# Scan outputs read from PSUM, a skip term made by channel, and softmax maps combined by ScalarE and GpSimd, in a hybrid SSD and attention block

## The chip, the cores and the metric

The kernel runs on one core of a Trainium2 chip. Its metric is device time in microseconds (us); lower is better. Three runs of the kernel before stand at 1765.82, 1765.89 and 1776.22 us.

## The reference

One layer of a backbone block: a modulated norm, one input projection, and two groups of heads that read it side by side, a bidirectional scan (SSD) and a differential attention. Both go into an output projection, and a gated MLP follows. What the change touches is this, cut to its core (8 chunks of 128 tokens, 2 groups of 8 scan heads, 4 attention heads with two maps each, 1024 queries over 1280 keys):

```python
# scan, per direction: y = intra-chunk part + state part + skip
y_diag = einsum('bclsgr,bcsgrp->bclgrp', scores * decay * dt, xs)
y_off  = einsum('bclgn,bcgrpn,bclgr->bclgrp', cm, h_starts, exp(a_cum))
yd     = y_diag + y_off + d_skip * xs
ys     = rmsnorm((yd_forward + yd_backward) * silu(z), ssd_norm_g)
# attention: two maps per head
p = softmax(q @ k * scale, axis=-1)
w = p[:, :, 0] - lam * p[:, :, 1]
o = w @ v
```

## The kernel before

The program is written as one stream in Python; what one engine does next is the order in which its instructions come out, and a scheduler may move them, except TensorE's in the stages where `pin` holds them in program order. Each engine works through its own queue in order.

After the startup and the input projection (to about 440 us) TensorE alternates between attention and a filler, by a debt that `run` keeps: each attention step yields a gap, and the filler is run until its costs (0.65, S_COST, M_COST) have paid for it. First the filler is `zproj`, the projection for z; when it is used up it is `ssd`, the scan. What is left of the scan when attention ends runs in `ssd_rest`, inside `mixffn`, beside the norm of the attention's output (tiles o, dg, yo). Then the output projection and the MLP follow to the end.

**Attention** goes by tiles of 128 queries of one head, 32 in all. For each of the two maps TensorE makes scores (tile sc, one buffer of three PSUM banks), VectorE takes their row maximum (stat), ScalarE the exponentials (et), and only then can TensorE write the next sc. One tile behind, `weigh` makes the map difference out of the two et tiles: a reciprocal, a 128x1 factor, and one VectorE instruction over 128x1280. TensorE transposes the result in ten blocks (tr), ScalarE or VectorE copies these out (wt), and after every second tile TensorE multiplies by V (po).

**The scan** runs 11 state steps first (`bwd`, `fwd`: GpSimd weighs x into xw and decays the state into hb or H, TensorE makes s, VectorE adds it), then `main(c, g)` for 8 chunks and 2 groups, with a state step between chunks. One such unit: the score product scs (for both groups at once, copied to sc by ScalarE), G = G * sc on VectorE, two state products yo (forward and backward), each copied out of PSUM by ScalarE and scaled by GpSimd, or scaled straight from PSUM by VectorE, by the letters of ENG_B (beside attention) and ENG_R (in the rest); the skip term xd = xt * dsum; two sums; eight small products y; yg = y + the sums; a transpose yt; and yt * z into zc, which goes to DRAM (yd). The PSUM pool pm has three buffers that scs, yo, y, yt and s take in turn.

The two lines of the loop around the change that words can't carry:

```python
nc.vector.scalar_tensor_tensor(out=ex[0], in0=ex[1], scalar=st[:, 6:7], in1=ex[0], op0=ALU.mult, op1=ALU.add)
e = [{"p": nc.gpsimd, "d": nc.vector}[x] for x in (ENG_R if self.rest else ENG_B)]   # "pdppdp", "ppppdp"
```

## Time and profile before

| | |
|---|---|
| median of three runs | 1765.89 us |
| the profiled execution | 1772.42 us |
| its span | 1770.5 us |
| TensorE busy | 1590.3 us (90%) |
| VectorE busy | 1206.5 us (68%) |
| GpSimd busy | 842.9 us (48%) |
| ScalarE busy | 758.9 us (43%) |
| DMA, mean | 154 GB/s |

The profile is one execution on the chip. A matmul in float32 shows as two instructions, so that "x16" is eight products. PE is TensorE, DVE VectorE, ACT ScalarE, POOL GpSimd, SP the engine that issues DMAs. "<- DVE x" behind an idle time names what ended it. In this text the stretch from 440 to 900 us is cut into four: the z projection beside attention (445 to 622 us, tiles 0 to 15), the state steps beside attention (622 to 730, tiles 16 to 23), the chunks beside attention (730 to 841, tiles 24 to 31), and the rest of the scan (841 to 897).

### The profile page before, as it was taken

The numbers are of one execution on the slowest core, as the hardware profiler recorded it, in microseconds if no ns is written. First come the engines' busy times: TensorE is split into PE (matmuls) and PEld (weight loads), VectorE is DVE, ScalarE is ACT, GpSimd is POOL, SyncE is SP. The second block draws the span as 40 slices with busy tenths as digits, with TensorE's granted clock in tenths as the row PEclk, the third lists the DMA queues.
The fourth block names the chain that finished last, engine by engine and source line by source line (L and its number), as shares of the span: only waits on it lengthen the run. The fifth ranks groups of instructions, "written<-read, shape, count | busy, mean of one in ns | idle before, by whom it ended". The sixth has DMA issues, their size and how long they took to land. (4 is left out here: it accounts for less than half of the span.)

```text
span 1770.5 us, 21306 instructions
## 1 busy us (share of the span) xinstructions
PE 1590.3 (90%) x7588; PEld 1271.8 (72%) x7588; DVE 1206.5 (68%) x1593; ACT 758.9 (43%) x1409; POOL 842.9 (48%) x559
## 2 busy tenths in 40 slices
PE   5899989997899978988899995999999999999986
PEld 2697877885687855666467774778888887777765
DVE  3478843354565657777875568987677777798886
ACT  4433577542354423444444254433334334355352
POOL 2231587784010045566756576343333334566642
PEclk8999999999899988999999997999999999999987
DMA  8365866766422284645564331323322225753222
GB/s 300 113 225 197 268 208 234 269 214 193 131 83 82 77 283 166 175 152 158 182 208 153 120 102 36 113 95 113 113 102 101 95 102 176 285 179 123 81 74 95
DMA packets 138825, 273.34 MB, mean 154 GB/s; under 512 B 11984, under 2 KB 60544, under 8 KB 138208
## 3 DMA queue, kind: packets, MB, share of 16 engines
q1 hardware_dynamic: 138128, 271.03, 46.2%
q8 instruction: 60, 0.98, 0.2%
q0 software_dynamic: 592, 0.96, 0.2%
q14 instruction: 45, 0.37, 0.1%
HBM read 197.63 MB, written 74.32 MB: 154 GB/s over the span
## 5 line engine op out<-in xcount | busy, mean ns | idle before, releaser
L145 PE MATMUL pu<-T,whi 128*128 128x512 f32 x1232 | 383.5, 392 | 8.7 <-ACT whi L125 8.7
L145 PEld LDWEIGHTS pu<-T,whi 128*128 128x128 f32 x1232 | 233.0, 189 | 57.6 <-ACT whi L125 9.2
L126 POOL TENSOR_TENSOR wlo<-S,whi 128x512 fp32r<-128x512 f32 (+2 forms) x122 | 167.0, 1373 | 192.8 <-ACT whi L125 192.6
L145 PE MATMUL pu<-T,wlo 128*128 128x512 f32 x616 | 242.5, 394 | 16.7 <-POOL wlo L126 11.8
L126 POOL TENSOR_TENSOR wlo<-wraw,whi 128x512 fp32r<-128x512 f32 (+2 forms) x118 | 152.2, 1294 | 163.3 <-ACT whi L125 156.3
L145 PE MATMUL lat<-hl,w_hi 128*128 128x512 f32 x640 | 206.2, 399 | 0.9 <-DVE dtt L599 0.9
L145 PE MATMUL pd<-T,whi 128*128 128x512 f32 x560 | 178.9, 400 | 11.6 <-ACT whi L125 7.4
L814 DVE TENSOR_REDUCE stat<-sc 128x1 f32<-128x1280 f32 x64 | 95.2, 1488 | 109.3 <-PE sc L145 109.2
L126 POOL TENSOR_TENSOR w_lo<-w_raw,w_hi 128x1024 fp32r<-128x1024 f32 (+1 forms) x36 | 81.8, 2275 | 179.3 <-ACT w_hi L125 157.6
L125 ACT CAST whi<-wraw 128x512 fp32r<-128x512 f32 (+2 forms) x140 | 81.3, 582 | 197.4 <-PE pu L145 118.9
L145 PEld LDWEIGHTS pu<-T,wlo 128*128 128x128 f32 x616 | 116.5, 189 | 45.2 <-POOL wlo L126 13.4
L145 PEld LDWEIGHTS lat<-hl,w_hi 128*128 128x128 f32 x640 | 122.9, 192 | 26.8 <-DVE dtt L599 1.1
L145 PE MATMUL sc<-K,S 128*128 128x512 f32 (+1 forms) x384 | 101.2, 401 | 45.1 <-DMA K<-kd 23.6
L815 ACT ACTIVATE et<-sc,stat 128x1280 f32<-128x1280 f32 x64 | 85.1, 1330 | 130.0 <-DVE stat L814 111.8
L145 PEld LDWEIGHTS pd<-T,whi 128*128 128x128 f32 x560 | 107.6, 193 | 37.8 <-ACT whi L125 9.6
L125 ACT CAST whi<-S 128x512 fp32r<-128x512 f32 (+2 forms) x144 | 81.6, 573 | 119.2 <-PE pu L145 88.4
L145 PEld LDWEIGHTS sc<-K,S 128*128 128x128 f32 x384 | 76.1, 207 | 72.9 <-ACT et L815 30.0
L145 PE MATMUL lat<-hl,w_lo 128*128 128x512 f32 x320 | 127.8, 399 | 0.0
L145 PE MATMUL pd<-T,wlo 128*128 128x512 f32 x280 | 113.3, 405 | 7.3 <-POOL wlo L126 7.1
L1409 DVE SCALAR_TENSOR_TENSOR xf<-pd,modl,xf 128x512 f32<-128x512 f32 (+1 forms) x138 | 95.9, 727 | 14.1 <-PE pd L145 10.8
L542 ACT ACTIVATE R<-R,lna 128x128 f32<-128x128 f32 x256 | 78.1, 391 | 53.7 <-POOL R L538 48.5
L538 POOL TENSOR_TENSOR R<-R,never 128x1024 f32<-128x1024 f32 x32 | 80.5, 2529 | 41.0 <-DMA R<-atd 39.0
(285 smaller groups left out, 3410.3 us busy)
## 6 DMA issues: line engine op xcount, KB each, us to landing
wraw<-wUp SPq DMA_DIRECT2D x46, 512.0 KB, 3.2
wt<-wmB SPq DMA_DIRECT2D x32, 512.0 KB, 4.1
R<-atd SPq DMA_DIRECT2D x32, 512.0 KB, 5.4
stg<-gf_d SPq DMA_DIRECT2D x21, 768.0 KB, 4.8
w_raw<-wU SPq DMA_DIRECT2D x28, 512.0 KB, 5.0
gf_d<-T SPq DMA_DIRECT2D x11, 1024.0 KB, 4.2
K<-kd SPq DMA_DIRECT2D x32, 320.0 KB, 7.6
xt<-xtok SPq DMA_DIRECT2D x19, 512.0 KB, 5.2
```

Of the source, the lines that this page charges most:

```text
L125: nc.scalar.copy(hi, src)
L126: (lo_eng or nc.vector).tensor_tensor(out=lo, in0=src, in1=hi, op=ALU.subtract)
L145: self.pe(self.nc.tensor.matmul(out, lhsT=lhsT, rhs=rhs, start=start, stop=stop))
L538: nc.gpsimd.tensor_tensor(out=R[:, d], in0=R[:, d], in1=self.never[:, d].unsqueeze(1).broadcast_to([P, 8, P]), op=ALU.add)
L542: nc.scalar.activation(e, e, AF.Exp, bias=self.lna[:, d, i, h:h + 1], scale=1.0)
L814: nc.vector.tensor_reduce(out=st[:, c:c + 1], in_=sc, axis=AX.X, op=ALU.max, negate=True)
L815: nc.scalar.activation(et, sc, AF.Exp, bias=st[:, c:c + 1], accum_out=acc)
L1409: nc.vector.scalar_tensor_tensor(out=o, in0=ps, scalar=self.gate5[:, dt:dt + 1], in1=o, op0=ALU.mult, op1=ALU.add)
```

## The change

Three things are changed. First, in the scan VectorE reads every product from PSUM itself: scs is made for each group apart and multiplied into G straight from PSUM, the backward yo is scaled into t, the forward yo is scaled in place and added to t, and yt is multiplied by z from PSUM. ScalarE's copies sc, t and yt are gone, and so are GpSimd's scalings and sums; ENG_B, ENG_R and the second t buffer go with them. Second, the skip term is no longer made by token in the scan: the convolved x is also stored by channel (xct), `zproj` loads its half (xc, one buffer), multiplies it by the skip factor of the channel and by the gate on VectorE and stores it (zx), and the scan loads zx and adds it to zc on GpSimd as its last step. Third, the maps are combined in two steps: ScalarE scales the second et in place, and GpSimd adds it to the first; the 128x1 factor is made by a tensor_scalar instead of a scalar_tensor_tensor. et has four buffers instead of three, wt three instead of four, and the last wt copy moves from VectorE to ScalarE (WT_ENG).

```diff
-ENG_B = "ppppdp"
-ENG_R = "pdppdp"
-WT_ENG = "aad"
+WT_ENG = "aaa"
...
+                    if u < U_B:
+                        nc.sync.dma_start(self.xct[u], y[:, CTX:])
...
+                xc = zp.tile([P, 512], F32, name="xc", bufs=1)
+                nc.sync.dma_start(xc, self.xct[u][:, sl])
                 zo = zp.tile([P, 512], F32, name="zo")
                 nc.scalar.activation(zo, p, AF.Tanh, scale=0.5)
                 nc.vector.scalar_tensor_tensor(out=zo, in0=zo, scalar=1.0, in1=p, op0=ALU.add, op1=ALU.mult)
                 nc.sync.dma_start(self.zt[u][:, sl], zo)
+                nc.vector.scalar_tensor_tensor(out=xc, in0=xc, scalar=self.dsum[:, u:u + 1], in1=zo,
+                                               op0=ALU.mult, op1=ALU.mult)
+                nc.sync.dma_start(self.zx[u][:, sl], xc)
...
-            et = ap.tile([P, TOK], F32, name="et", bufs=3)
+            et = ap.tile([P, TOK], F32, name="et", bufs=4)
...
-            nc.vector.scalar_tensor_tensor(out=st[:, 6:7], in0=st[:, 5:6], scalar=self.nlam[:, 0:1],
-                                           in1=self.s0[:, qt, h:h + 1], op0=ALU.mult, op1=ALU.mult)
-            nc.vector.scalar_tensor_tensor(out=ex[0], in0=ex[1], scalar=st[:, 6:7], in1=ex[0], op0=ALU.mult, op1=ALU.add)
+            nc.vector.tensor_scalar(out=st[:, 6:7], in0=st[:, 5:6], scalar1=self.nlam[:, 0:1],
+                                    scalar2=self.s0[:, qt, h:h + 1], op0=ALU.mult, op1=ALU.mult)
+            nc.scalar.mul(ex[1], ex[1], st[:, 6:7])
+            nc.gpsimd.tensor_tensor(out=ex[0], in0=ex[0], in1=ex[1], op=ALU.add)
...
+            zx = sp.tile([P, 4, P], F32, name="zx", bufs=Z_BUFS)
+            nc.sync.dma_start(zx, self.zx[ks, :, cs].rearrange("k p t -> p k t"))
...
+                ps = self.pm.tile([P, P], F32, tag="mm", name="scs")
+                self.mm(ps, bl[:, g, :], cl[:, g, :])
+                nc.vector.tensor_tensor(out=G, in0=ps.unsqueeze(1).broadcast_to([P, 8, P]), in1=G, op=ALU.mult)
+                t = sp.tile([P, 8, HD], F32, name="t")
+                for d, st in ((1, hb), (0, self.Hf)):
                     po = self.pm.tile([P, 512], F32, tag="mm", name="yo")
                     self.mm(po, cl[:, g, :], st[:, xg])
-                    if e[d] is nc.gpsimd:
-                        nc.scalar.copy(t.rearrange("p h d -> p (h d)"), po)
-                    src = t if e[d] is nc.gpsimd else h3(po)
+                    nc.vector.tensor_tensor(out=t if d else h3(po), in0=h3(po), in1=ea, op=ALU.mult)
+                    if d == 0:
+                        nc.vector.tensor_tensor(out=flat(t), in0=po, in1=flat(t), op=ALU.add)
...
-            e.tensor_tensor(out=zc, in0=y, in1=zc, op=ALU.mult)
+            nc.vector.tensor_tensor(out=zc, in0=pt, in1=zc, op=ALU.mult)
+            nc.gpsimd.tensor_tensor(out=zc, in0=zc, in1=zx, op=ALU.add)
```

How this moves the queues shows at three places. Line numbers of the changed kernel are its own.

VectorE, one chunk beside attention, before (TENSOR_REDUCE is the maximum of an sc, et<-et the map difference):

```order
L814 TENSOR_REDUCE stat<-sc 128x1
L976 TENSOR_TENSOR G<-G,sc 128x1024 x2
L835 COPY wt_6056<-tr 128x2x128
L820 RECIPROCAL stat<-stat 128x1
L821 SCALAR_TENSOR_TENSOR stat<-stat,nlam,s_95 128x1
L823 SCALAR_TENSOR_TENSOR et<-et,stat 128x1280
L814 TENSOR_REDUCE stat<-sc 128x1
L994 TENSOR_TENSOR t_6082<-t_6082,xd 128x512
L999 TENSOR_TENSOR yg<-y,t_6082 128x512
```

VectorE, the same place in the changed kernel, the first of the chunk's two units:

```order
L819 TENSOR_REDUCE stat<-sc 128x1 x2
L978 TENSOR_TENSOR G<-scs,G 128x1024
L985 TENSOR_TENSOR t<-yo,acum 128x512
L985 TENSOR_TENSOR yo<-yo,acum 128x512
L825 RECIPROCAL stat<-stat 128x1
L987 TENSOR_TENSOR t<-yo,t 128x512
L826 TENSOR_SCALAR stat<-stat,nlam,s_95 128x1
L993 TENSOR_TENSOR yg<-y,t 128x512
L1005 TENSOR_TENSOR zc<-yt,zc 128x512
L978 TENSOR_TENSOR G<-scs,G 128x1024
L819 TENSOR_REDUCE stat<-sc 128x1
```

Five instructions of a unit read PSUM where two and a half did, the 128x1280 instruction is gone, and between two maxima there now stands a whole unit.

GpSimd, one chunk beside attention, before (xw and H are the state step):

```order
L914 TENSOR_TENSOR H_6408<-H_6205,cd 128x1024
L986 TENSOR_TENSOR t_6285<-t_6285,acum 128x512
L986 TENSOR_TENSOR t_6294<-t_6294,acum 128x512
L993 TENSOR_TENSOR t_6285<-t_6285,t_6294 128x512
L1016 TENSOR_TENSOR zc<-yt,zc 128x512
L986 TENSOR_TENSOR t_6337<-t_6337,acum 128x512
L991 TENSOR_TENSOR xd<-xt,c_dskp 128x512
L986 TENSOR_TENSOR t_6342<-t_6342,acum 128x512
L1016 TENSOR_TENSOR zc<-yt,zc 128x512
L993 TENSOR_TENSOR t_6337<-t_6337,t_6342 128x512
L908 TENSOR_TENSOR xw<-xt,dte 128x1024
```

GpSimd, one chunk beside attention in the changed kernel:

```order
L920 TENSOR_TENSOR H_6674<-H_6480,cd 128x1024
L829 TENSOR_TENSOR et<-et 128x1280
L1006 TENSOR_TENSOR zc<-zc,zx 128x512
L829 TENSOR_TENSOR et<-et 128x1280
L1006 TENSOR_TENSOR zc<-zc,zx 128x512
L914 TENSOR_TENSOR xw<-xt,dte 128x1024
```

Ten small instructions of the scan have become two, and two additions of 128x1280 for the attention have come in.

VectorE beside the z projection, in the changed kernel (before, zo stands there without xc, and et<-et after the 128x1 factor):

```order
L825 RECIPROCAL stat<-stat 128x1
L826 TENSOR_SCALAR stat<-stat,nlam,s_95 128x1
L123 TENSOR_TENSOR wt_4306<-tr,wt_4305 128x2x128
L775 SCALAR_TENSOR_TENSOR zo<-zo,pz 128x512
L777 SCALAR_TENSOR_TENSOR xc<-xc,c_dskp,zo 128x512
L819 TENSOR_REDUCE stat<-sc 128x1 x2
```

The product xc has come in ahead of a maximum. On the queue of DMAs, a store of zx has come in between the first zt and the loads of the first head's S and K.

## Rows read from the trace of the kernel before

**Rows 1.** Busy time per stretch; columns: stretch, length, PE, PEld, DVE, ACT, POOL, granted clock, DMA share, GB/s

```profile
445.00:622.00 177.00, 164.88 (x888) 138.72 (x886) 109.22 (x139) 79.59 (x134) 10.60 (x4) 0.96 0.32 94
622.00:730.00 108.00, 85.19 (x348) 60.53 (x349) 72.08 (x77) 35.85 (x60) 54.49 (x29) 0.86 0.70 217
730.00:841.00 111.00, 98.49 (x520) 75.88 (x520) 86.90 (x85) 47.96 (x83) 74.64 (x55) 0.97 0.49 156
841.00:897.00 56.00, 46.00 (x213) 25.93 (x211) 46.09 (x68) 25.53 (x54) 38.88 (x27) 0.97 0.49 158
```

**Rows 2.** TensorE's waits from 440 to 900 us: total, times, longest

```profile
PE sc L145 <- DMA K<-kd: 23.6, 6, 10.5
PE sc L145 <- ACT et L815: 21.0, 13, 3.3
PE yt L1010 <- DVE yg L999: 9.2, 7, 3.7
```

**Rows 3.** VectorE's groups from 440 to 900 us, shapes apart: busy, mean ns, idle before

```profile
L814 DVE TENSOR_REDUCE stat<-sc 128x1 f32<-128x1280 f32 x64 | 95.2, 1488 | 109.3 <-PE sc L145 109.2
L823 DVE SCALAR_TENSOR_TENSOR et<-et,stat 128x1280 f32<-128x1280 f32 x32 | 61.1, 1908 | 0.6
L994 DVE TENSOR_TENSOR t<-t,xd 128x512 f32<-128x512 f32 x16 | 24.1, 1505 | 7.7 <-POOL t L993 7.7
L976 DVE TENSOR_TENSOR G<-G,sc 128x1024 f32<-128x1024 f32 x16 | 23.9, 1534 | 4.9 <-ACT sc L973 4.9
...
L821 DVE SCALAR_TENSOR_TENSOR stat<-stat,nlam,s 128x1 f32<-128x1 f32 x32 | 16.7, 521 | 0.9
L999 DVE TENSOR_TENSOR yg<-y,t 128x512 f32<-128x512 f32 x16 | 10.9, 682 | 0.5
```

**Rows 4.** Timeline, two engines at 789.7 us: start, length, instruction

```profile
789.66 1.90 POOL L914 TENSOR_TENSOR H<-H,cd 128x1024 f32<-128x1024 f32 x1
790.09 1.48 DVE L821 SCALAR_TENSOR_TENSOR stat<-stat,nlam,s 128x1 f32<-128x1 f32 x1
```

**Rows 5.** Timeline of TensorE, one pair of tiles, from 767 to 796 us

```profile
767.83 1.47 PE L145 MATMUL sc<-K,S 128*128 128x512 f32 x6 [2.23 <-ACT et L815]
...
776.11 1.41 PE L145 MATMUL sc<-K,S 128*128 128x512 f32 x6
777.36 1.02 PE L145 MATMUL yo<-H,cl 128*128 128x512 f32 x2
...
779.08 1.98 PE L145 MATMUL y<-xt,G 128*128 128x64 f32 x16
781.59 0.66 PE L1010 MATMUL yt<-c_masks,yg 128*128 128x128 f32 x4 [0.53 <-DVE yg L999]
782.00 1.41 PE L145 MATMUL sc<-K,S 128*128 128x512 f32 x6
...
784.12 1.88 PE L145 MATMUL s<-xw,btk 128*128 128x512 f32 x4
...
786.50 1.43 PE L145 MATMUL sc<-K,S 128*128 128x512 f32 x6 [0.28 <-ACT et L815]
787.77 4.48 PE L145 MATMUL po<-wt,V 128*128 128x256 f32 x20
794.48 1.43 PE L145 MATMUL sc<-K,S 128*128 128x512 f32 x6 [2.23 <-ACT et L815]
```

**Rows 6.** GpSimd's groups, shapes apart, whole span: busy, mean ns, idle before

```profile
L126 POOL TENSOR_TENSOR w_lo<-w_raw,w_hi 128x1024 fp32r<-128x1024 f32 x28 | 70.0, 2502 | 172.2 <-ACT w_hi L125 150.4 <-PE tr L831 21.7
...
L1016 POOL TENSOR_TENSOR zc<-yt,zc 128x512 f32<-128x512 f32 x16 | 20.8, 1302 | 7.5 <-ACT yt L1013 7.5
```

**Rows 7.** ScalarE's exponential, a group of its own, from 100 to 920 us

```profile
L815 ACT ACTIVATE et<-sc,stat 128x1280 f32<-128x1280 f32 x64 | 85.1, 1330 | 130.0 <-DVE stat L814 111.8 <-DMA K<-kd 16.8
```

**Rows 8.** Timeline at 555 us: a tile's reciprocal, and its first transposes

```profile
555.10 0.17 DVE L820 RECIPROCAL stat<-stat 128x1 f32<-128x1 f32 x1 [0.23 <-ACT et L815]
...
562.36 0.82 PE L831 MATMUL tr<-c_masks,et 128*128 128x128 f32 x6
```

More of the change, by code (lines that the diff above doesn't have):

```diff
@@ L61 @@
 Z_BUFS = 2
-T_BUFS = 2
 S_COST = 3.4
@@ L259, in build @@
             self.pa = self.pool(e_pa, "pa", 2, space=PSUM)
-            self.pin, self.rest = True, False
+            self.pin = True
             at = self.attention(att)
@@ L271, in ssd_rest @@
             def ssd_rest():
-                self.rest = True
                 for _ in sd:
@@ L343, in consts @@
         self.zt = self.dp.tile([KT, P, SEQ], F32, name="zt")
+        self.xct = self.dp.tile([KT, P, SEQ], F32, name="xct")
+        self.zx = self.dp.tile([KT, P, SEQ], F32, name="zx")
         self.gd = self.dp.tile([NL, NG, P, 8, P], F32, name="gd")
@@ L385, in late_loads @@
         self.dtb = ld("dtb", [P, 32], bc("dtb"))
-        self.dsk = ld("dskp", [P, 2, NH], io["dskp"].broadcast_to([P, 2, NH]))
+        self.dsk = ld("dskp", [P, 2, KT], io["dskp"])
         lamv = self.lamv = cp.tile([P, 4, QK], F32, name="lamv")
@@ L877, in attention @@
                 if m % 2 == 0:
-                    wt = [[ap.tile([P, 4, 256], F32R, name=f"wt{s}", bufs=4) for s in range(2)] for _ in range(3)]
+                    wt = [[ap.tile([P, 4, 256], F32R, name=f"wt{s}", bufs=3) for s in range(2)] for _ in range(3)]
                 for gi in range(2):
@@ L966, in go @@
                 xg = slice(g * 512, (g + 1) * 512)
-                e = [{"p": nc.gpsimd, "d": nc.vector}[x] for x in (ENG_R if self.rest else ENG_B)]
-                if g == 0:
-                    ps = self.pm.tile([P, NG, P], F32, tag="mm", name="scs")
-                    for gg in range(NG):
-                        self.mm(ps[:, gg, :], bl[:, gg, :], cl[:, gg, :])
-                    sc = sp.tile([P, NG, P], F32, name="sc")
-                    nc.scalar.copy(sc, ps)
-                    chunk[c, "s"] = sc
-                    yield M_COST * 0.44
@@ L976, in go @@
-                nc.vector.tensor_tensor(out=G, in0=G, in1=chunk[c, "s"][:, g, :].unsqueeze(1).broadcast_to([P, 8, P]),
-                                        op=ALU.mult)
-                ts = []
-                for d, st in ((0, self.Hf), (1, hb)):
+                flat = lambda t: t.rearrange("p h d -> p (h d)")
+                ps = self.pm.tile([P, P], F32, tag="mm", name="scs")
+                self.mm(ps, bl[:, g, :], cl[:, g, :])
+                nc.vector.tensor_tensor(out=G, in0=ps.unsqueeze(1).broadcast_to([P, 8, P]), in1=G, op=ALU.mult)
@@ L980, in go @@
+                yield M_COST * 0.22
+                t = sp.tile([P, 8, HD], F32, name="t")
+                for d, st in ((1, hb), (0, self.Hf)):
                     po = self.pm.tile([P, 512], F32, tag="mm", name="yo")
                     self.mm(po, cl[:, g, :], st[:, xg])
-                    t = sp.tile([P, 8, HD], F32, name=f"t{d}", bufs=T_BUFS)
-                    if e[d] is nc.gpsimd:
-                        nc.scalar.copy(t.rearrange("p h d -> p (h d)"), po)
-                    src = t if e[d] is nc.gpsimd else h3(po)
@@ L986, in go @@
-                    e[d].tensor_tensor(out=t, in0=src, in1=self.ea[:, d, i, 8 * g:8 * g + 8].unsqueeze(2)
-                                       .broadcast_to([P, 8, HD]), op=ALU.mult)
-                    ts.append(t)
-                    yield M_COST * 0.85
-                xd = sp.tile([P, 8, HD], F32, name="xd")
-                e[2].tensor_tensor(out=xd, in0=h3(xt[:, xg]), in1=self.dsum[:, 8 * g:8 * g + 8].unsqueeze(2)
-                                   .broadcast_to([P, 8, HD]), op=ALU.mult)
@@ L993, in go @@
-                e[3].tensor_tensor(out=ts[0], in0=ts[0], in1=ts[1], op=ALU.add)
-                e[4].tensor_tensor(out=ts[0], in0=ts[0], in1=xd, op=ALU.add)
+                    ea = self.ea[:, d, i, 8 * g:8 * g + 8].unsqueeze(2).broadcast_to([P, 8, HD])
+                    nc.vector.tensor_tensor(out=t if d else h3(po), in0=h3(po), in1=ea, op=ALU.mult)
+                    if d == 0:
+                        nc.vector.tensor_tensor(out=flat(t), in0=po, in1=flat(t), op=ALU.add)
+                    yield M_COST * 0.85
@@ L998, in go @@
                 yg = sp.tile([P, 512], F32, name="yg")
-                nc.vector.tensor_tensor(out=yg, in0=y, in1=ts[0].rearrange("p h d -> p (h d)"), op=ALU.add)
-                late.append((yg, zc, ks, cs, e[5]))
+                nc.vector.tensor_tensor(out=yg, in0=y, in1=flat(t), op=ALU.add)
+                late.append((yg, zc, zx, ks, cs))
                 yield M_COST * 0.85
@@ L1006, in finish @@
         def finish():
-            yg, zc, ks, cs, e = late.pop(0)
+            yg, zc, zx, ks, cs = late.pop(0)
             pt = self.pm.tile([P, 4, P], F32, tag="mm", name="yt")
@@ L1010, in finish @@
                 self.pe(nc.tensor.transpose(pt[:, q, :], yg[:, q * P:(q + 1) * P], self.ident))
-            if e is nc.gpsimd:
-                y = sp.tile([P, 4, P], F32, name="yt")
-                nc.scalar.copy(y, pt)
-            else:
-                y = pt
-            e.tensor_tensor(out=zc, in0=y, in1=zc, op=ALU.mult)
+            nc.vector.tensor_tensor(out=zc, in0=pt, in1=zc, op=ALU.mult)
+            nc.gpsimd.tensor_tensor(out=zc, in0=zc, in1=zx, op=ALU.add)
             nc.sync.dma_start(self.yd[ks, :, cs].rearrange("k p t -> p k t"), zc)
@@ L1614, in layouts @@
     a["dtb"] = g("dt_bias")[0].reshape(1, 32)
-    a["dskp"] = g("d_skip")[0][None]
+    a["dskp"] = np.repeat(g("d_skip")[0], HD, axis=1).reshape(2, KT, P).transpose(2, 0, 1)
     for n, s in (("lq1", "lam_q1"), ("lk1", "lam_k1"), ("lq2", "lam_q2"), ("lk2", "lam_k2")):
```

2 lines of the change are left out of this document (1 added, 1 removed).

## The prediction

> **What bounds the kernel now.** I read the busy shares first: TensorE is busy 90% of the span, so a change on other engines can only give back TensorE's idle time, and it has to be found by stage. The change reaches four stretches; the reader is to see in each how long TensorE was idle [rows 1]: 12.1 us in 445 to 622 (177.0 less 164.88), 22.8 in 622 to 730, 12.5 in 730 to 841, 10.0 in 841 to 897, together 57.4. The clock is granted at 0.96 to 0.97 in three of them and at 0.86 in the second, where TensorE is busy least (79%). So 57 us is the most that removing idle time can give there, plus something for the clock in the second stretch.
>
> Then I read what TensorE waits for [rows 2]. 23.6 us are for K to land at a new head; the change removes none of it. 21.0 us are for ScalarE's exponentials, which free the one score buffer. 9.2 are for yg on VectorE. Behind the exponentials stands VectorE's queue, and there the groups [rows 3] show means that their shapes don't explain: t<-t,xd takes 1.505 us where yg, of the same 128x512, takes 0.682; a 128x1 factor takes 0.521. The timeline shows why: the factor at 790.09 lasts 1.48 us and ends with GpSimd's H, which began at 789.66 and took 1.90 [rows 4]. [...] The price in one pair of tiles: the four intervals between score blocks are 8.3, 5.9, 4.5 and 8.0 us, 26.65 in all [rows 5]. 4.5 is the bare loop, with products s in between; in the last one the products po end at 792.25, and the scores come at 794.48, for the maximum was held up behind the blocked factor.
>
> **The change, part by part.**
>
> *The combination of the maps.* VectorE loses 32 instructions of 1.908 us, 61 us, and the blocked part of the factor: 32 times 0.521 less about 0.2 (a 128x1 reciprocal takes 0.17 [rows 8]), some 10 us more. [...] ScalarE gains 32 times 1.33 us (the exponential of the same shape, from PSUM, [rows 7]), 43 us on an engine that is 43 to 45% busy in these stretches (79.59 of 177, 47.96 of 111 [rows 1]). GpSimd gains 32 additions of 128x1280. No row shows one; 128x512 with two full inputs takes 1.302 and 128x1024 takes 2.502 [rows 6], so the same slope gives 3.1 us, 99 us in all; the bounds are 2.5 (the 1024 row) and 3.3 (two and a half times the 512 row).
>
> What hides this longer chain is the lag of one tile. Before, from the reciprocal to the finished map it took 0.2 + 0.2 + 1.9, 2.3 us; now 0.2 + 0.2 + 1.3 + 3.1, 4.8 with nothing queued ahead. From the reciprocal at 555.10 to the first transposes at 562.36 there are 7.3 us [rows 8]. So the cover is 2.5 us. One weight split on GpSimd ahead (2.5 us) uses it up, and two state instructions (1.90 each [rows 4]) overdraw it by 1.3. In the first stretch only weight splits are there, one in two tiles; beside the state steps it is overdrawn at times. Cost at nothing in the first and third stretch, 1.5 us a tile in the second, counted there.
>
> *The skip term.* It adds 8 stores (xct), 16 loads (xc), 16 stores and 16 loads (zx), some 17 MB; the DMA share is 0.32 in the first stretch and 0.49 in the last two [rows 1], so bandwidth is there, and only beside the state steps (0.70) it is tight. At the first head the zx store waits for VectorE ahead of the loads of S and K, for which TensorE then waits up to 10.5 us [rows 2]: one VectorE product (0.68) and one more issue, 1 us late, and up to 3.8 if GpSimd holds the product. I take 1. In the first stretch xc stands ahead of a maximum, 0.68 us where TensorE has nothing to spare, 14 times, and it has both inputs in SBUF. Against it the 128x1280 instruction has left that place. Net I take 2 us of loss, from 3 of gain to 14 of loss (1 us at each).
>
> *The scan's outputs.* Per unit VectorE has G from PSUM and five instructions of 128x512. G lies between 1.36 (twice yg) and 1.53 (today's mean); I take 1.36, since a PSUM input was not held up in yg. The unit costs 1.36 + 5 times 0.68, 4.8 us; today 1.53 + 1.51 + 0.68, 3.7, and 0.7 more where it scales a yo. Per pair of tiles, which holds one chunk, that adds 2.2 us and the maps' combination takes away 2 times 1.9 and two factors' blockage: VectorE ends at or below today's 78% (86.90 of 111.00). What matters is the order. I laid one pair out with the starts of [rows 5]. First interval: scores and eight transposes 2.1 (782.00 to 784.12), two yo 1.7 (777.36 to 779.08), y 2.0, yt 0.4 (781.59 to 782.00), two scs and two transposes some 0.9: 7.1 us for 8.3. Second: scores 1.25 (776.11 to 777.36), two yo, y and yt: 5.3 for 5.9, since yt no longer waits 0.53 for yg. Third: 4.5 as now. Fourth: scores 1.25 and po 4.48, 5.7 for 8.0. In the first two, 12.4 us, VectorE has two units and two maxima of 1.49 [rows 3], 12.6 with the lengths as recorded, and back to back somewhat less; so it only just keeps up, and each PSUM buffer comes free in time. That is 22.6 us for 26.65, and TensorE has hardly a gap left in it. Over four pairs this would be 16; the stretch's idle time is 12.5 and other pairs may be shorter now, so I take 10, from 0 to 12.5.
>
> *The state steps, 622 to 730.* Of 22.8 us idle up to 13 may be for K (23.6 less the 10.5 of the first head [rows 2], which lies before). In the remaining the maximum waits behind 128x1280 instructions that GpSimd stretches. Per tile 1.9 to 3 us of VectorE go, 1.5 come back by the late addition; GpSimd rises from 54.49 us to 54 + 8 times 3.1, 79 of some 98, and nearly sets the pace. Seven full tiles of now 13 us at 1.4 less: 10 us, from 3 (half of it and twice the delay by the additions) to 20 (nearly all idle time, or less of it with some clock).
>
> *The rest, 841 to 897.* TensorE is busy 46.0, VectorE 46.09 of 56. There VectorE gains six units at 4.8 against 4.4 with the yo scaling, but its waits for GpSimd go, and the chain through three engines becomes one engine's. I take 4.5 us, from 0 (VectorE as full as before) to 9.
>
> *The sum:* 1 + 2 - 10 - 10 - 4.5 = -21.5 us. The profiled execution took 1772.4 us, 6.5 above the median of 1765.9; its sum gives 1751, and against the median 1744.4. The parts after 897 us keep their instructions.
>
> **The rivals.** *Slower:* the product xc is held up by GpSimd. For it speaks that it has both inputs in SBUF, like the instructions of [rows 3], and that GpSimd, nearly idle in the first stretch (10.60 us), now works 16 additions there, 50 us. If each of the 16 half-units paid a whole addition on TensorE's path, 3.1 us, that is 50 us against a gain of 24.5 elsewhere and 1 at K: 1792. It decides from 1.5 us per half-unit. Against it: an addition fills 28% of that stretch, and the maximum often waits for scores anyway. [...]
>
> *No difference:* VectorE is now the only reader of five PSUM tiles with three buffers, and the maxima queue behind whole units. If the third and fourth stretch gain nothing, 1 + 2 - 10 leaves 1759. For it: in the rest VectorE is already as busy as TensorE. Against it: the pair as laid out.
>
> *More:* TensorE closes up entirely. 57.4 less the K waits that lie in these stretches, 13, is 44: 1722. For it: the pair as laid out has no gap. Against it: the stretch of the state steps rests on GpSimd's pace.
>
> That the change does not do what it says is ruled out by the queues: the instructions are gone from them.
>
> **How the numbers follow.** Forecast 0.50 (its own range 1732 to 1756), no difference 0.24, more 0.15, slower 0.11. The range leaves out the slow rival and half of a tenth on the fast side: 1718 to 1770. One per cent (17.7 us) is about what a measurement here can tell from no change. Faster by it means below 1748: 0.7 of the forecast, all of more, a little of no difference, 0.56. Slower 0.11. The rest, 0.33, is within.
>
> **What would show it.** Right: et<-et gone from VectorE's queue, the 128x1 factor near 0.2 us, G and the products from PSUM near 1.36 and 0.68 whatever GpSimd does; score intervals of a pair near 22.6; TensorE's idle time in 730 to 841 under 5 us; transposes waiting for GpSimd only beside the state steps. Wrong: xc with a mean well over 1.5 us, or TensorE waiting for et from GpSimd in the first stretch; GpSimd's additions over 3.3 us; TensorE waiting on VectorE for PSUM buffers in the rest, with VectorE above 90% there.

## The result, and the profile after

The changed kernel takes 1744.63 us (median of four runs) beside 1769.29 for the kernel before, a ratio of 0.9864 (95% interval 0.9822 to 0.9906). A second comparison, on another occasion, gave 1743.17 beside 1764.94, ratio 0.9859 (0.9834 to 0.9884). By the first interval that is 17 to 31 us less, by the second 20 to 29. Forecast were 1744 and 21.5 us less.

To see where the time went I cut both kernels at the same events: the first exponential of tiles 0, 16 and 24, the last exponential of tile 31, and the first product of the output projection (pw). The stretches then follow the work and not the clock. They are those of [rows 1] but for a few microseconds at their ends, and but for one border: the chunks end here with the last exponential (824.7 us in the first profile before) and in [rows 1] 16 us later, with the last products po of the attention. Cut there, the gains are the same to 0.2 us (-11.7 and -5.7). Both kernels were profiled twice (the second profiles are e1 and e9 below).

| stretch, us | before | after | difference of means |
|---|---|---|---|
| start to tile 0 | 447.2, 447.1 | 436.4, 436.2 | -10.9 |
| tiles 0 to 15 (z projection) | 175.6, 175.9 | 180.5, 181.1 | +5.1 |
| tiles 16 to 23 (state steps) | 107.1, 101.7 | 100.5, 99.6 | -4.4 |
| tiles 24 to 31 (chunks) | 94.8, 94.6 | 83.0, 82.9 | -11.8 |
| rest of the scan, to pw | 72.8, 74.6 | 68.2, 67.9 | -5.6 |
| pw to the end | 873.0, 873.6 | 874.6, 874.3 | +1.1 |
| span | 1770.5, 1767.5 | 1743.1, 1741.9 | -26.5 |

The largest single item but one lies ahead of everything that the prediction spoke of.

Busy time of the changed kernel in its four stretches (columns as in [rows 1]):

```profile
436.37:616.91 180.54, 163.13 (x882) 136.91 (x880) 97.24 (x137) 101.21 (x150) 57.25 (x20) 0.97 0.43 133
616.91:717.36 100.45, 80.31 (x342) 56.97 (x343) 48.14 (x66) 45.68 (x68) 65.63 (x31) 0.88 0.74 233
717.36:800.35 82.99, 80.40 (x442) 64.18 (x442) 58.35 (x79) 43.18 (x64) 44.40 (x23) 0.98 0.63 200
800.35:868.55 68.20, 61.58 (x301) 38.05 (x300) 54.28 (x96) 23.87 (x47) 21.51 (x14) 1.00 0.62 198
```

In the chunks TensorE is idle 2.6 of 83.0 us. Between the same events before it was idle 11.2 of 94.8:

```profile
729.86:824.71 94.85, 83.60 (x439) 64.85 (x439) 75.02 (x73) 42.30 (x74) 60.54 (x44) 0.96 0.47 148
```

VectorE is busy 70% of the chunks now and GpSimd 53%. Beside the state steps 20 us of idle time are left, at a granted clock of 0.88. What TensorE waits for now, from 430 to 890 us (answers [rows 2]; total, times, longest):

```profile
PE sc L142 <- DMA K<-kd: 27.6, 9, 11.0
PE sc L142 <- ACT et L820: 8.2, 8, 3.0
PE tr L837 <- DVE wt L123: 6.8, 6, 2.5
PE tr L837 <- POOL et L829: 5.0, 5, 2.0
PE s L142 <- DVE hb L928: 4.9, 2, 3.6
PE yt L1004 <- DVE yg L993: 2.3, 1, 2.3
```

The wait for the exponentials fell from 21.0 to 8.2 us and that for yg from 9.2 to 2.3. The waits for K grew by 4.0, of which 0.5 are the first head's. New are the transposes that wait for GpSimd's additions (5.0), and those that wait for VectorE's wt copies take 6.8 us where they took 3.8 (the kernel before):

```profile
PE tr L831 <- DVE wt L126: 3.8, 6, 0.7
```

VectorE's groups of the same window, shapes apart, answer [rows 3]:

```profile
L819 DVE TENSOR_REDUCE stat<-sc 128x1 f32<-128x1280 f32 x64 | 95.3, 1489 | 130.9 <-PE sc L142 130.8
...
L978 DVE TENSOR_TENSOR G<-scs,G 128x1024 f32<-128x1024 f32 x16 | 19.4, 1214 | 3.9 <-PE scs L142 3.9
L777 DVE SCALAR_TENSOR_TENSOR xc<-xc,c_dskp,zo 128x512 f32<-128x512 f32 x15 | 12.6, 838 | 2.6 <-DMA xc<-xct 2.4
L985 DVE TENSOR_TENSOR yo<-yo,acum 128x512 f32<-128x512 f32 x16 | 11.0, 689 | 2.5 <-PE yo L142 2.5
...
L1005 DVE TENSOR_TENSOR zc<-yt,zc 128x512 f32<-128x512 f32 x16 | 11.0, 686 | 5.0 <-PE yt L1004 2.1 <-DMA zc<-zt 2.1 <-issue 0.6
...
L826 DVE TENSOR_SCALAR stat<-stat,nlam,s 128x1 f32<-128x1 f32 x32 | 8.7, 271 | 0.8
```

In each unit six instructions of VectorE read PSUM (G, t, yo in place, the sum of the two, yg, zc), where beside attention one did (yg). In the means each has the length of its shape, 0.68 to 0.69 for 128x512 and 1.21 for G, and the factor takes 0.27 where its mean was 0.52. The new work on the other two engines, from the same view:

```profile
L829 POOL TENSOR_TENSOR et<-et 128x1280 f32<-128x1280 f32 x32 | 93.5, 2921 | 128.4 <-ACT et L828 121.7 <-issue 6.7
```

```profile
L828 ACT ACTIVATE et<-et,stat 128x1280 f32<-128x1280 f32 x32 | 43.7, 1366 | 16.7 <-DVE stat L826 16.7
```

And one pair of tiles on TensorE's timeline, which answers [rows 5]:

```profile
753.92 1.51 PE L142 MATMUL sc<-K,S 128*128 128x512 f32 x6
...
760.62 1.41 PE L142 MATMUL sc<-K,S 128*128 128x512 f32 x6
...
765.67 1.40 PE L142 MATMUL sc<-K,S 128*128 128x512 f32 x6
...
770.20 1.42 PE L142 MATMUL sc<-K,S 128*128 128x512 f32 x6 [0.32 <-ACT et L820]
771.47 4.48 PE L142 MATMUL po<-wt,V 128*128 128x256 f32 x20
775.59 1.51 PE L142 MATMUL sc<-K,S 128*128 128x512 f32 x6
```

The four intervals are 6.7, 5.05, 4.5 and 5.4 us, 21.7 for 26.65, with one gap of 0.3 us in it.

### The profile page after: what moved, and what is told of

It is laid out like the page before. It is cut to its first block, busy times and chain, and to the rows that moved or that the text cites. A ratio compares the mean times of both kernels' runs of the same rounds, so it can differ in the third digit from the quotient of the medians.

```text
span 1743.1 us, 21450 instructions
## 1 busy us (share of the span) xinstructions
PE 1583.1 (91%) x7588; PEld 1268.2 (73%) x7588; DVE 1152.9 (66%) x1607; ACT 782.2 (45%) x1403; POOL 855.1 (49%) x533
## 5 line engine op out<-in xcount | busy, mean ns | idle before, releaser
L829 POOL TENSOR_TENSOR et<-et 128x1280 f32<-128x1280 f32 x32 | 93.5, 2921 | 128.4 <-ACT et L828 121.7
L122 ACT CAST whi<-S 128x512 fp32r<-128x512 f32 (+2 forms) x144 | 81.8, 573 | 121.1 <-PE pu L142 90.2
L142 PE MATMUL sc<-K,S 128*128 128x512 f32 (+1 forms) x384 | 98.1, 391 | 36.1 <-DMA K<-kd 27.6
L820 ACT ACTIVATE et<-sc,stat 128x1280 f32<-128x1280 f32 x64 | 85.1, 1330 | 86.9 <-DVE stat L819 65.1
```

Source lines behind the costliest of these rows:

```text
L122: nc.scalar.copy(hi, src)
L142: self.pe(self.nc.tensor.matmul(out, lhsT=lhsT, rhs=rhs, start=start, stop=stop))
L820: nc.scalar.activation(et, sc, AF.Exp, bias=st[:, c:c + 1], accum_out=acc)
L829: nc.gpsimd.tensor_tensor(out=ex[0], in0=ex[0], in1=ex[1], op=ALU.add)
```

## Experiments

Twelve runs, in three groups; two of them (e1, e9) repeat the kernels before and after. The times of the stretches, from one profile of each:

| | to tile 0 | tiles 0-15 | 16-23 | 24-31 | rest | from pw | median, us | ratio to before (95%) |
|---|---|---|---|---|---|---|---|---|
| e1 before again | 447.1 | 175.9 | 101.7 | 94.6 | 74.6 | 873.6 | 1769.42 (one run) | |
| e2 maps only | 446.2 | 172.1 | 92.6 | 104.3 | 77.5 | 872.4 | 1764.40 | 0.9993 (0.9973-1.0014) |
| e3 scan only | 444.0 | 175.6 | 104.3 | 98.1 | 72.7 | 869.5 | 1766.64 | 1.0015 (0.9998-1.0032) |
| e4 skip only | 436.3 | 185.0 | 103.2 | 86.0 | 69.9 | 872.6 | 1756.13 | 0.9950 (0.9931-0.9968) |
| e5 scan and maps | 450.8 | 173.2 | 92.3 | 82.7 | 69.0 | 873.5 | 1738.43 | 0.9842 (0.9813-0.9870) |
| e6 stores xct only | 436.0 | 174.5 | 101.8 | 94.4 | 71.2 | 869.5 | 1757.28 | 0.9960 (0.9929-0.9992) |
| e7 xc on GpSimd | 434.2 | 179.1 | 94.3 | 84.8 | 69.5 | 873.9 | 1736.95 | 0.9839 (0.9800-0.9878) |
| e8 factor as before | 437.4 | 179.1 | 100.9 | 81.3 | 67.2 | 870.2 | 1734.35 | 0.9828 (0.9801-0.9855) |
| e9 after again | 436.2 | 181.1 | 99.6 | 82.9 | 67.9 | 874.3 | 1743.17 | 0.9859 (0.9834-0.9884) |
| e10 e5 with e6 | 436.0 | 173.1 | 94.2 | 85.8 | 72.0 | 872.8 | 1736.70 | 0.9830 (0.9809-0.9850) |
| e11 e7, xc loaded early | 439.0 | 178.0 | 89.6 | 81.3 | 68.9 | 868.8 | 1728.67 | 0.9782 (0.9761-0.9803) |
| e12 sum on VectorE | 437.8 | 187.2 | 97.5 | 85.5 | 72.3 | 870.5 | 1749.68 | 0.9897 (0.9872-0.9921) |

The kernel before had a median of 1764.72 us (25 runs, 1756.68 to 1772.32) beside e1 to e4, 1765.08 beside e5 to e8 and 1764.94 beside e9 to e12.

### Each part alone: e1 to e4

The theory was the prediction's: VectorE held up by GpSimd, and chains across engines, were what TensorE waited for. The rival was VectorE's load as such.

*e1_before_again*, no edit. 

> The kernel before once more, for its profile. In the two profiles compared so far the first exponential of the attention starts at 447.2 us before and at 436.4 after, 10.8 us earlier, although the work ahead of it is the same but for eight stores. If that is the order of the queues, which the change also re-sorted there, it starts here at 447 again, within 1.5. If it is a difference between executions of the same program, it starts somewhere else, down to 437. Both expect the stretches behind it as before, within 2 us: 175.6 for tiles 0 to 15, 107.1 for tiles 16 to 23, 94.8 from there to the last exponential.

The first exponential came at 447.1, so the 10.9 us are no accident of one execution. Tiles 16 to 23 took 5.4 us less than in the first profile; differences of that size between executions of one program have to be allowed for there. TensorE's busy time makes all of it (85.1 and 79.0 us), at a granted clock of 0.86 and 0.92. Behind pw, where TensorE's queue is the same in all fourteen profiles, the times lie between 868.8 and 874.6.

*e2_maps_only*, the third part on the kernel before:

```diff
-            nc.vector.scalar_tensor_tensor(out=ex[0], in0=ex[1], scalar=st[:, 6:7], in1=ex[0], ...)
+            nc.scalar.mul(ex[1], ex[1], st[:, 6:7])
+            nc.gpsimd.tensor_tensor(out=ex[0], in0=ex[0], in1=ex[1], op=ALU.add)
```

> The kernel before with the third part alone (maps combined by ScalarE and GpSimd, four et and three wt buffers, all last wt copies on ScalarE). Theory, that what counts is VectorE held up by GpSimd: GpSimd then has 74.6 + 8 times 2.9, 98 us of work in the stretch of the chunks that lasts 95 to the last exponential, G and t<-t,xd on VectorE still stand still under it, and the transposes wait for the additions: no gain there, -3 to +6 us, and -4 to -8 in tiles 16 to 23: total -8 to +2. Rival, that VectorE's load counts and GpSimd has room: VectorE loses as much as in the full change, so the chunks gain 10 to 12 us and the total is -16 to -20. Ahead of the attention the queues are in the order of before: the first exponential within 1.5 us of the run of the kernel before, if order decides.

The time didn't move (the theory's total), and the stretches say why: tiles 0 to 15 gained 3.6 us and 16 to 23 gained 11.9, and the chunks lost 9.6, more than the theory allowed, and the rest 3.8. In the chunks (710.84 to 815.11 us) these are TensorE's waits, the busy times and one of VectorE's groups:

```profile
PE yt L1011 <- DVE yg L1000: 10.3, 4, 3.6
```

```profile
710.84:815.11 104.27, 88.10 (x447) 68.04 (x447) 53.62 (x59) 53.71 (x89) 82.84 (x53) 0.93 0.44 139
```

```profile
L995 DVE TENSOR_TENSOR t<-t,xd 128x512 f32<-128x512 f32 x8 | 10.3, 1286 | 9.2 <-POOL t L994 9.2
```

VectorE is busy only half the time, so its load isn't the cause. It stands 9.2 us for the sum t that GpSimd makes, which is now queued with the additions; yg comes late, and yt waits 10.3 us for it. Of the 9.6 us about half is idle time of TensorE (16.2 us for 11.2) and half busy time (88.1 for 83.6), at a granted clock of 0.93 for 0.96.

*e3_scan_only*, the first part, with the skip term by token:

```diff
+                xd = sp.tile([P, 8, HD], F32, name="xd")
+                nc.gpsimd.tensor_tensor(out=xd, in0=h3(xt[:, xg]), in1=self.dsum[:, 8 * g:8 * g + 8].unsqueeze(2)
+                                        .broadcast_to([P, 8, HD]), op=ALU.mult)
...
+                        nc.vector.tensor_tensor(out=flat(t), in0=po, in1=flat(t), op=ALU.add)
+                        nc.vector.tensor_tensor(out=t, in0=t, in1=xd, op=ALU.add)
```

> The kernel before with the first part alone (scan outputs read by VectorE from PSUM; the skip term still by token, its product on GpSimd and its sum on VectorE). Theory: GpSimd falls to some 45 us in the stretch of the chunks, so the 128x1280 map difference and the factor meet it less often, G is not held up, and yg comes sooner; but VectorE has 2.2 us a pair more and the sum with xd with both inputs in SBUF: chunks -3 to -8 us, rest -2 to -5, total -5 to -13. Rival, VectorE's load: chunks slower by 2.2 to 4 us a pair, 9 to 16 in all, total +5 to +12. Both: nothing in tiles 0 to 23.

Neither: the chunks became 3.4 us slower, the theory had them faster and the rival slower by 9 to 16. Their waits and VectorE's two groups for the maps (723.93 to 822 us):

```profile
PE sc L145 <- ACT et L815: 7.9, 7, 1.8
```

```profile
L823 DVE SCALAR_TENSOR_TENSOR et<-et,stat 128x1280 f32<-128x1280 f32 x7 | 15.6, 2235 | 0.1
...
L821 DVE SCALAR_TENSOR_TENSOR stat<-stat,nlam,s 128x1 f32<-128x1 f32 x7 | 4.2, 607 | 0.1
```

With GpSimd busy 27.3 of 98.1 us the 128x1280 instruction still takes 2.24 and the factor 0.61: what counts is which instruction stands beside them, not GpSimd's total. Two of the seven places, on the timeline of both engines:

```profile
748.25 1.54 DVE L823 SCALAR_TENSOR_TENSOR et<-et,stat 128x1280 f32<-128x1280 f32 x1
748.41 2.28 POOL L973 TENSOR_TENSOR xd<-xt,c_dskp 128x512 f32<-128x512 f32 x1 [8.62 <-DVE t L983]
...
760.99 1.90 POOL L914 TENSOR_TENSOR H<-H,cd 128x1024 f32<-128x1024 f32 x1
761.08 3.16 DVE L823 SCALAR_TENSOR_TENSOR et<-et,stat 128x1280 f32<-128x1280 f32 x1
```

Where VectorE begins first, it takes 1.54 and GpSimd's xd takes 2.28 (1.04 where nothing stands beside it); where GpSimd's H begins 0.09 us earlier, VectorE takes 3.16. The latter happened three times. VectorE is then busy 81.8 us, and the scores go on waiting for the exponentials (7.9).

*e4_skip_only*, the second part:

```diff
+                        nc.sync.dma_start(self.xct[u], y[:, CTX:])
...
+                nc.vector.scalar_tensor_tensor(out=xc, in0=xc, scalar=self.dsum[:, u:u + 1], in1=zo, ...)
+                nc.sync.dma_start(self.zx[u][:, sl], xc)
```

> The kernel before with the second part alone (skip term by channel, with three wt buffers to make room). Its queues ahead of the attention are re-sorted as in the changed kernel. If the order makes the 10.8 us, the first exponential starts at 436 to 438 here; if it was one execution's chance, anywhere within 437 to 447, as in the other kernels. Tiles 0 to 15: theory +3 to +6 us, for the product xc waits out a weight split on GpSimd once (1.9 us where it takes 0.75) and TensorE's clock falls to the lower level behind that; xc alone costs 16 times 0.75 at most, 12. Chunks: VectorE loses 8 sums of 1.5 us and GpSimd the products xd: -3 to -6. Total -2 to +2 without the 10.8, -9 to -13 with it.

Start at 436.3, tiles 0 to 15 longer by 9.3, chunks shorter by 8.7, both beyond the theory's +3 to +6 and -3 to -6. The skip part alone brings 8.6 us, just short of the -9 to -13 and less than its earlier start.

### Parts together, and the sites of loss: e5 to e8

*e5_scan_maps*: the edits of e2 and e3 in one kernel. 

> The kernel before with the first and the third part, without the second (skip term by token, its product on GpSimd, its sum on VectorE). Alone they gave +1.9 and -0.3 us. Theory: the two need each other, since the scan's move to VectorE frees GpSimd for the additions (in the chunks it has some 45 us of its own and 23 of additions, 70 of 95, where the maps alone made it 98), and the additions' move takes the blocked 128x1280 from VectorE. Tiles 0 to 15 as in the maps alone, 172; 16 to 23 from 92 to 101; chunks 83 to 89, with the sum of xd on VectorE for the difference to the full change's 83.0; the rest from 68 to 72; ahead of the attention 444 to 447, since the queues there are in the order of before. Total 1738 to 1750. Rival, that parts add up: 1766, with chunks at 103 to 107.

Two parts that alone are worth +1.9 and -0.3 us are worth 26 together. The chunks show it as two by two: 94.7 with neither, 104.3 with the maps, 98.1 with the scan, 82.7 with both. The scan frees GpSimd for the additions, and the additions free VectorE for the scan. This kernel's median is also 5 to 6 us below the changed one's, though it starts the attention later; the runs of the two overlap (1733.68 to 1743.20, and 1736.75 to 1746.53), so no more than that can be said of the total. In the profiles the changed kernel takes 7.6 us longer in tiles 0 to 15 and 7.7 in 16 to 23, and the skip term saves nothing in the chunks once the other two are there.

*e6_xct_only*, the kernel before with eight stores that nobody reads:

```diff
+                    if u < U_B:
+                        nc.sync.dma_start(self.xct[u], y[:, CTX:])
+                    else:
```

> The kernel before with nothing but the eight stores xct, whose data nobody reads. TensorE's queue up to the first scores then stands in the order of the changed kernel, but for two rows early on that stand as before. Theory, that the re-sorted queue makes the 10.8 us ahead of the attention: the first exponential at 440 to 443, since of the 10.8 us some 4.5 arise by 82 us, where those two rows stand, and some 6 between 170 and 320, where the stores stand; total 1757 to 1761. Rivals: the re-sort by the stores gives all of it, 436 and 1754; or none, and what the skip term's other edits do gives all, 447 and 1765. All: nothing after the first exponential beyond 2 us.

In the profile it is the first rival: the stores give all of the earlier start. In the timed runs less of it is seen: the median is 7.8 us below the kernel before, in the theory's range, the ten runs lie between 1747.62 and 1769.74, and the profiled one (1749.14) is among the fastest; it is also 4 us shorter than the mean before from pw on, where nothing was edited. The stores take DMA time (512 KB each, 3.9 us from issue to landing in the median, in the changed kernel) and do no work, which speaks for the order that the queues take around them (of the 2145 matmul records that TensorE's trace has ahead of the first scores 247 stand elsewhere). No kernel had the stores in the old order, so this much is argued. TensorE's waits for the transposes of the convolved x (ptr), from 150 to 330 us, first in e1, then in e6:

```profile
PE ptr L619 <- ACT st L620: 9.6, 4, 4.5
```

```profile
PE ptr L621 <- DVE st L622: 6.1, 2, 4.4
```

In the old order (e1, e2, e3, e5 and the first profile) this wait is 9.4 to 11.9 us, in the new (all others) 4.4 to 6.2. From the first product pc to the last ptr it is 203.5 us in e1 and 192.8 in e6, with the clock at 0.96 and 0.98: 3.9 us less idle and 6.9 less busy time. The first exponential lies between 444.0 and 450.8 us in the five profiles of the old order, and between 434.2 and 439.0 in the nine of the new.

*e7_xc_gpsimd*:

```diff
-                nc.vector.scalar_tensor_tensor(out=xc, in0=xc, scalar=self.dsum[:, u:u + 1], in1=zo, ...)
+                nc.scalar.mul(xc, xc, self.dsum[:, u:u + 1])
+                nc.gpsimd.tensor_tensor(out=xc, in0=xc, in1=zo, op=ALU.mult)
```

> The changed kernel with the product xc taken off VectorE: ScalarE scales xc by the skip factor, GpSimd multiplies it by the gate. Tiles 0 to 15 take 180.5 us in the changed kernel and 172.1 with the maps alone. Theory, that xc in VectorE's queue makes these 8 us, by its own 0.75 us ahead of a maximum, by the one long wait for a weight split and by what TensorE's clock loses behind it: 172 to 175, total 1736 to 1740 where the changed kernel has 1744.6. Rival, that the added loads and stores make them, by K's landing later and by SP's queue: 178 to 182, total 1743 to 1748. GpSimd has 16 instructions of 1.3 us more beside 57 of 187, so the additions come late at most once a tile and by 1.3 us, within the 2.5 us of slack.

The median is in the theory's range, but its interval overlaps those of the changed kernel. The place is the theory's only in part: tiles 16 to 23 gave 5.7 us, tiles 0 to 15 just 1.8, and the chunks took 1.9 more. In tiles 0 to 15 most pairs are 0.3 to 3 us shorter, but tile 7 took 18.1 us where the changed kernel has 11.9: ahead of an exponential ScalarE stood for xc, whose load was queued behind the second head's S and K (timeline of ScalarE):

```profile
526.36 0.72 ACT L777 ACTIVATE xc<-xc,c_dskp 128x512 f32<-128x512 f32 x1 [4.29 <-DMA xc<-xct]
526.99 1.31 ACT L820 ACTIVATE et<-sc,stat 128x1280 f32<-128x1280 f32 x1
```

*e8_factor_stt*:

```diff
-            nc.vector.tensor_scalar(out=st[:, 6:7], in0=st[:, 5:6], scalar1=..., scalar2=self.s0[:, qt, h:h + 1], ...)
+            nc.vector.scalar_tensor_tensor(out=st[:, 6:7], in0=st[:, 5:6], scalar=..., in1=self.s0[:, qt, h:h + 1], ...)
```

> The changed kernel with the 128x1 factor made by a scalar_tensor_tensor again, so with two inputs in SBUF; nothing else. In the changed kernel the tensor_scalar lies over a GpSimd instruction in 8 of 32 tiles and takes 0.27 us in every one. Theory: in those 8 tiles it takes 0.9 to 1.5 us again, VectorE loses about 1 us in each of the four pairs of chunks, where it only just keeps up, and the chunks go from 83.0 to 85 to 88, total +2 to +6. Rival, that a pair has room for it: the factor takes as long, but the chunks stay within 1 us, total within 2.

The hold-up came back and cost nothing that the chunks show. The same place in the changed kernel and in e8 (timelines; GpSimd's xw, then VectorE's factor):

```profile
726.61 1.91 POOL L914 TENSOR_TENSOR xw<-xt,dte 128x1024 f32<-128x1024 f32 x1 [5.20 <-PE s L142]
...
727.37 0.28 DVE L826 TENSOR_SCALAR stat<-stat,nlam,s 128x1 f32<-128x1 f32 x1
```

```profile
724.81 1.90 POOL L914 TENSOR_TENSOR xw<-xt,dte 128x1024 f32<-128x1024 f32 x1 [3.34 <-PE s L142]
...
725.56 1.17 DVE L826 SCALAR_TENSOR_TENSOR stat<-stat,nlam,s 128x1 f32<-128x1 f32 x1
```

In the changed kernel the factor begins 0.76 us into xw and takes 0.28. In e8 it begins 0.75 into xw and lasts until xw ends, 1.17. It took 1.16 to 1.24 in six tiles, and the chunks took 81.3 us. The rival is right: the pair has the room. That the total is 9 us below e9 is not the factor's doing as far as the stretches show: of the 5.8 us between the two profiles 4.1 lie behind pw, where TensorE's queue is the same, and the two intervals overlap. It stays open.

### Controls and combinations: e9 to e12

*e9_after_again*, no edit. 

> The changed kernel once more, on the chip of the three below, for the spread of its time (so far four runs from 1736.8 to 1746.5) and of its stretches. Tiles 0 to 15 at 179 to 182, 16 to 23 at 99 to 103 if the late load of xt there belongs to the queue's order, anything from 93 if it was one execution's; chunks 81 to 84; total 1736 to 1745.

All stretches within 1 us of the first profile of the changed kernel, so the late state steps there belong to the program.

*e10_scan_maps_xct*: e5 with the stores of e6. 

> The kernel before with the first and third part, the skip term by token, and the eight stores xct that nobody reads, for the order that they give to the queues ahead of the attention. Theory, that the second part is worth its re-sorted queue and costs some 15 us in the attention: both gains add up, first exponential at 434 to 438, tiles 0 to 15 at 172 to 174, 16 to 23 at 92 to 94, chunks 82 to 84, rest 68 to 70; total 1725 to 1731, faster than the changed kernel by 10 to 16. Rival, that an early start is given back (K lands no earlier, so TensorE waits for it): 1735 to 1740.

The start is at 436.0, but the total is the rival's: 1736.7, no difference from e5 beyond the intervals. Its profile loses 2 to 3 us each in tiles 16 to 23, in the chunks and in the rest against that of e5; K, the rival's reason, makes 2.8 us of waits there and 1.9 in e5, so that it explains less than one. The profiled execution of e5 is the slowest of its four, that of e10 the fastest of its four, so the stretches don't speak for the medians here. Where the earlier start went in the timed runs is not settled.

*e11_xc_early*, e7 with the load of xc ahead of the half-unit's products:

```diff
+                xc = zp.tile([P, 512], F32, name="xc")
+                nc.sync.dma_start(xc, self.xct[u][:, sl])
                 for k in range(KT):
...
-                zo = zp.tile([P, 512], F32, name="zo")
+                zo = zp.tile([P, 512], F32, name="zo", bufs=1)
```

> The changed kernel with the product xc on ScalarE and GpSimd, and with xc loaded a half-unit ahead (two buffers for xc, one for zo). In the version with one buffer ScalarE stood 4.3 us ahead of an exponential for a load that was queued behind the second head's S and K, and the pair there took 6 us longer. Theory: this wait goes, tiles 0 to 15 at 172 to 175, 16 to 23 at 92 to 95, total 1728 to 1733. Rival, that the wait is for K and comes whatever xc does: 178 to 181 and 1736 to 1739.

At 1728.67 us this is the fastest kernel of the study, 14 us below the changed one in the same comparison, and its interval (0.9761 to 0.9803) doesn't meet that of e9. But the wait that it was made for is still there (timeline of ScalarE), tile 7 takes 17.8 us, and tiles 0 to 15 the rival's 178.0:

```profile
530.02 0.72 ACT L777 ACTIVATE xc<-xc,c_dskp 128x512 f32<-128x512 f32 x1 [2.49 <-DMA xc<-xct]
```

The queue put this load behind S and K again; the buffer only moved which half-unit it serves. In the profiles the gain on e9 lies in tiles 16 to 23 (89.6 for 99.6) and from pw on (868.8 for 874.3); the second can't be put down to the edit, since the queue there is the same.

*e12_add_vector*:

```diff
-            nc.gpsimd.tensor_tensor(out=ex[0], in0=ex[0], in1=ex[1], op=ALU.add)
+            nc.vector.tensor_tensor(out=ex[0], in0=ex[0], in1=ex[1], op=ALU.add)
```

> The changed kernel with the sum of the two maps on VectorE; ScalarE still scales, GpSimd is nearly idle. Theory, that a pair of chunks leaves VectorE no room: the sum takes 1.4 us where GpSimd is idle and up to 3 where it meets xw or H, so a pair goes from 21.7 to 24 to 27 us and the chunks from 83 to 90 to 100; tiles 0 to 15 lose 0 to 5; total 1750 to 1768. Rival, that with little on GpSimd VectorE is not held up and 1.4 us a tile fit in: chunks at 82 to 86, total within 4 us of the changed kernel.

The chunks took 85.5 us, a pair 23.1: the rival's number, VectorE has most of the room for it. The total is neither's, 6.5 us above e9 and just below the theory's 1750. Tiles 0 to 15 took 187.2, 6.1 more than e9, beyond either. There the sum takes 1.49 us of VectorE in each tile, and 2.2 and 2.3 in the two where it met a weight split. In the chunks it takes 1.79 in the mean, and VectorE is busy 70.0 of 85.5 us, where it was 81.8 of 98.1 in e3. So with the sum on VectorE, too, most of the gain in the chunks is there. Which of the differences between e3 and this kernel makes it, the shorter map instruction (1.79 for 2.24), the factor or the sum with xd that is gone, was not tried apart.

## Why the prediction came out right, point by point

**The total was right in part by a term that it didn't have.** Its five terms made -21.5; the same five measured -16.2 (0.5 for the first K, 11.0 us for 10.5, and 5.1 - 4.4 - 11.8 - 5.6). What fills the gap is -11.4 ahead of that K, and 1.1 is lost after pw. The step that failed is "It adds 8 stores (xct) ... so bandwidth is there": the stores were costed as bytes, and what they bring about in the queues of the input projection has no term. That the median, 1744.63, lies so close to the 1744.4 forecast is luck: this gain made up for the state steps and the skip term.

**The combination of the maps.** The addition took 2.92 us (3.1 forecast, 2.5 to 3.3), ScalarE's product 1.37 (1.33), the factor 0.27. The cover held in the main: of the 5.0 us that TensorE waited for GpSimd, 3.0 lie beside the state steps, where the forecast had them, but 1.0 lie in tiles 0 to 15 and 1.1 behind the chunks, where it had none. The addition takes 1.96 times what it takes on VectorE in e12 where nothing holds it (1.49). On VectorE it costs more here all the same: 6.5 us by the medians of e9 and e12, whose runs don't overlap.

**The factor.** It is no longer held up, as forecast: in eight tiles it ran while a GpSimd instruction did, and it took 0.26 to 0.28. A hold-up does show in a larger tensor_scalar of the same kernel, dg over 128x128, which takes 0.28 us alone and here lasts to the end of GpSimd's weight split (timelines of VectorE and GpSimd in the changed kernel):

```profile
911.13 1.09 DVE L221 TENSOR_SCALAR dg<-c_masks,rcol 128x128 f32<-128x128 f32 x1
```

```profile
910.64 1.50 POOL L123 TENSOR_TENSOR w_lo<-w_raw,w_hi 128x512 fp32r<-128x512 f32 x1 [0.21 <-ACT w_hi L122]
```

As a scalar_tensor_tensor the factor is held up: in the first profile before, 14 of the 32 began while a GpSimd instruction ran, took 0.48 to 1.48 us and ended with it to 0.02 us, where the other 18 took 0.21 to 0.22; in e8 it ends with xw to 0.02 us. What decides which instruction is held up, the place of its inputs among it, from which the prediction argues, was not tried by itself. That this hold-up costs time, which the reading of the last interval of [rows 5] supposed, is refuted by e8 for the changed kernel; in the kernel before it was not tried.

**The skip term.** 2 us of loss were taken, 5.1 measured, 7.6 by e5 and the mean of the two profiles after. The slow rival's mechanism is real, once: xc met a weight split (timeline of the changed kernel, all engines), and TensorE's clock is granted at 0.66 from 489 to 494 us, a mean of 0.50 (490 to 492) and 1.00 (493 to 494):

```profile
484.18 2.36 POOL L123 TENSOR_TENSOR w_lo<-w_raw,w_hi 128x1024 fp32r<-128x1024 f32 x1 [3.29 <-ACT w_hi L122]
...
485.21 1.89 DVE L777 SCALAR_TENSOR_TENSOR xc<-xc,c_dskp,zo 128x512 f32<-128x512 f32 x1
...
487.01 1.27 DVE L123 TENSOR_TENSOR wt<-tr,wt 128x512 fp32r<-128x512 f32 x2
...
487.75 0.44 PE L837 MATMUL tr<-c_masks,et 128*128 128x128 f32 x2 [2.50 <-DVE wt L123]
...
489.63 2.34 PE L142 MATMUL sc<-K,S 128*128 128x512 f32 x6
```

```profile
484.00:489.00 5.00, 2.50 (x16) 1.85 (x14) 4.96 (x7) 3.21 (x7) 2.36 (x1) 1.00 0.36 112
489.00:494.00 5.00, 5.00 (x25) 4.47 (x24) 1.55 (x2) 1.53 (x2) 2.91 (x1) 0.66 0.50 153
```

xc lasts 1.89 for 0.75, the copies wt behind it end 2.5 us too late for the transposes, and the scores that follow take 2.34 us for 1.3. It never met an addition for longer than 0.4 us, so the 3.1 per half-unit of that rival didn't come about: the loss is 0.5 us per half-unit, a third of the point from which it decides.

**The chunks and the rest.** The pair was laid out at 7.1, 5.3, 4.5 and 5.7 us and came to 6.7, 5.05, 4.5 and 5.4: the eight products y take 1.73 us from their start to the next instruction's (2.0 taken), and two scs with two transposes 0.6 (0.9). VectorE's G took 1.21 (1.36). -11.8 for -10, and -5.6 for -4.5; up to the forecast's border TensorE is idle 3.8 us, with under 5 forecast. "No difference" rested on VectorE being the only reader of five PSUM tiles; TensorE waited for it 3.2 us in all in the rest, and VectorE is busy 80% there (54.28 of 68.20; 85% from the forecast's border on).

**The state steps.** -10 was forecast from GpSimd's pace, -4.4 came, and GpSimd was busy 65.6 of 100.5 us where the forecast had 79 of some 98. Without the skip term the stretch takes 92.6 and 92.3 us in e2 and e5, 12 less than the mean before. 8 of these come back in the changed kernel, e8 and e9. Of the 8.2 between e5 and the first profile of the changed kernel 4.8 are TensorE's busy time, at a granted clock of 0.88 for 0.94, and 3.4 are idle. What differs is the order of GpSimd's queue. In the changed kernel an addition stands between an xw and a decay hb of the state steps, and s waits 3.6 us for hb (TensorE's waits above). In e5 hb comes ahead of the addition, and s waits 1.3 (timelines of GpSimd, first the changed kernel, then e5):

```profile
643.18 1.90 POOL L914 TENSOR_TENSOR xw<-xt,dte 128x1024 f32<-128x1024 f32 x1 [4.70 <-issue]
645.04 2.91 POOL L829 TENSOR_TENSOR et<-et 128x1280 f32<-128x1280 f32 x1
647.91 1.90 POOL L920 TENSOR_TENSOR hb<-hb,cd 128x1024 f32<-128x1024 f32 x1
```

```profile
647.59 1.90 POOL L909 TENSOR_TENSOR xw<-xt,dte 128x1024 f32<-128x1024 f32 x1 [3.00 <-issue]
649.45 1.91 POOL L915 TENSOR_TENSOR hb<-hb,cd 128x1024 f32<-128x1024 f32 x1
651.31 2.90 POOL L824 TENSOR_TENSOR et<-et 128x1280 f32<-128x1280 f32 x1
```

The eight profiles with the additions on GpSimd divide by this order: the changed kernel, e8 and e9 take 99.6 to 100.9 us, and e2, e5, e7, e10 and e11, with hb ahead, 89.6 to 94.3. e7 and e11 have the skip term, so its work alone doesn't cost the 8 us. That the order does is what the traces suggest; a kernel that changes only this order was not tried.
